# One 512-column width for two output products, modulation sums of two groups at a time, pool factors loaded ahead, low parts last

## The chip, the core and the metric

The kernel runs on one core of a Trainium2 chip. Its engines are PE (TensorE, matrix products; PEld is its weight load), DVE (VectorE), ACT (ScalarE), POOL (GpSimd) and SP (SyncE, which here only issues DMAs). Each runs its own program in order and waits for others by semaphores. The metric is device time in microseconds of one execution; lower is better. Before the change it is 2888.54 us (median of 3 runs, 2886.82 to 2889.20).

## What is computed

All arrays are float32. `first_block` runs two layers over two streams, 256 tokens of `x` and 256 of `ctx`, 2048 wide; the second layer returns only `x`. `second_block` then works on 256 tokens. Cut to what matters here:

```python
for l in range(2):
    sh, sc, g = split(silu(c) @ w_mod[l] + b_mod[l], 3)       # and the same of c_ctx, for the stream ctx
    parts = split((x * (1 + sc) + sh) @ w_in[l])              # cu cb cc cg q k v ag pu pg
    ...                                                       # attention, short convolution
    # pool, four groups, window w = 2, 4, 8, 16:
    mean = (csum[hi] - csum[lo]) / (hi - lo)                  # the divisors depend on the position alone
    y_pool = silu(pg) * (((mean - pu) @ pool_w[l]) * pool_scale[l])
    out = concat(y_conv, y_attn, y_pool) @ w_out[l]           # 2048 x 2048
    x = layernorm(ALPHA * x + g * out, ln_g[l], ln_b[l])
z = rms_norm(x) @ w_in_2                                      # second block: two kinds of attention, gates
x = x + merged @ w_out_2                                      # 2048 x 2048
x = x + square(relu(rms_norm(x) @ w_up_2)) @ w_down_2
return rms_norm(x)
```

## The kernel before

**Products.** A float32 number is carried as two fp32r parts, `hi` and `lo` (the rest), and a product is the sum of three: high by high and both cross terms. Weights come from HBM on SP's queue in chunks of 512 KB (128 x 1024 numbers, `fetch`, L181), some chunks ahead of use; for each, ACT makes `hi` (L184) and DVE makes `lo` (L185). `wget` hands out the next chunk.

`lin_a` keeps a tile of 128 tokens as the stationary operand and streams weight columns past it; for each chunk and tile it calls `mm3` for each of the chunk's rows of 128 (k). `lin_b` keeps weights as the stationary operand, four blocks of 128 columns a product, and streams the activations. With both streams (512 tokens) it calls `mm3`. With 256 tokens ("fold") it streams the activations' high and low parts side by side, 512 columns, past the weights' high part (L266), and then 256 columns past the weights' low part (L268). All matrix products of layer 1 and of block 2 that go through `lin_b` are of this kind: 368 chunks with eight such pairs each, in 50 products.

**Output products.** `BLOCKS` cuts the 2048 output columns of `w_out` (both layers), `w_out_2` and the last quarter of `w_down_2` into three blocks of 512 and two of 256. A 512-column chunk holds two k, a 256-column chunk four. `mix_out` consumes each block on DVE with three operations for each token tile (L830 to L832: times the gate, plus the residual, statistics), and after the last block computes the layer norm's factors and starts the next layer (its turns by PE at L947, scale and shift L952 and L954, split into high and low L350 and L351, and POOL's rows L1014 and L1015). In layer 0 that is four tiles, in layer 1 and in block 2 two.

**Modulation sums.** `silu(c) @ w_mod` for later layers is summed beside other work: `mod_side` reads a group of 512 columns in eight chunks; DVE multiplies and adds for each k and stream (L416, L418, into the tiles `ma0` and `ma1`), and when all 16 k are in, PE adds over the partitions with a matrix of ones (`cols` L428 or `gate` L446: one 32-row float32 matmul for each stream). `cols` has a copy and four transposes behind it (L430, L435), `gate` an addition for each stream and two DMAs. Ten calls of `cols` and eight of `gate` go this way, the last four of `gate` for one stream alone (`side2`, layer 1's gate for `x`). What is `deferred` runs some side steps later (a step a chunk), wherever in the product that is.

**Pool stage.** `do_pu` builds window sums on DVE, loads the 1/count factors with a DMA on ACT's queue for each of the four groups (L628), multiplies and subtracts into `tmp` tiles (L631, L632), and defers a float32 product with `pool_w` on PE (L636) by 3+b side steps.

A scheduler with a cost model of its own orders each engine's instructions; the program's text gives the dependencies and the buffers.

Of the kernel before, what the change touches and what calls it, by code (L numbers as in the profile page):

```python
# [19 lines left out]
P = 128  # L20
# [41 lines left out]
def tile_two_blocks(ctx: ExitStack, tc: tile.TileContext, a: dict, out: bass.AP, blocks: dict):  # L62
# [14 lines left out]
    p_qs = pool("qs", 10)  # L77
# [167 lines left out]
    def mm3(ps, lh, ll, rh, rl, start, stop):  # L245
        mm(ps, lh, rh, start=start, stop=False)  # L246
        mm(ps, lh, rl, start=False, stop=False)  # L247
        mm(ps, ll, rh, start=False, stop=stop)  # L248

    def lin_b(act, tok, consume, ncols=512, korder=K16, mid=None):  # L250
# [6 lines left out]
        for k0 in korder:  # L257
            hi, lo = wget()
            last = k0 == korder[-1]
            nk = hi.shape[1]  # L260
            for (c, w), p in zip(nb, ps):
                for kk in range(nk):
                    ah, al = act[k0 + kk]
                    start, stop = k0 == korder[0] and kk == 0, last and kk == nk - 1
                    if fold:
                        mm(p[:w, :].rearrange("p (a t) -> p a t", a=2), hi[:, kk, c:c + w], act.both(k0 + kk, tok),  # L266
                           start=start, stop=False)
# [3 lines left out]
                if last:  # L271
                    consume(c // P, (p[:w].rearrange("p (a t) -> p t a", a=2),) if fold else p[:w, :ntok])
            side()
            bg_step()
            if mid:
                mid(k0)

    def lin_a(act, tiles, consume, korder=K16, mid=None, hold=1, lead=0, hook=None):
# [4 lines left out]
        for ks in [korder[:lead]][:lead] + [[k] for k in korder[lead:cut]] + [korder[cut:]]:  # L283
# [5 lines left out]
            for i, t in enumerate(tiles):  # L289
                for k0, (hi, lo) in zip(ks, ws):  # L290
                    nk, n = hi.shape[1:]
                    for kk in range(nk):
                        ah, al = act[k0 + kk]
# [109 lines left out]
    def mod_side(l, nt, streams=(0, 1), wait=5):  # L403

        st = {}

        def fn(k0):
            def step(raw):
                if k0 == 0:
                    for s in streams:  # L410
                        st[s] = p_ma.tile([P, 512], F32, tag=f"ma{s}", name=f"ma{s}")
                for kk in range(CHUNK):
                    k = k0 + kk
                    for s in streams:
                        if k == 0:
                            V.tensor_scalar(st[s], raw[:, kk, :], cc2[:, k, s:s + 1], None, op0=ALU.mult)  # L416
                        else:
                            V.scalar_tensor_tensor(st[s], raw[:, kk, :], cc2[:, k, s:s + 1], st[s], op0=ALU.mult,  # L418
                                                   op1=ALU.add)
                if k0 == K16[-1]:  # L420
# [3 lines left out]

        def cols():
            ps = aux()
            for s in streams:
                mm(ps[32 * s:32 * s + 32, :], ones, st[s], start=True, stop=True)  # L428
            r = st[0][:64]
            S.copy(r, ps[:64])  # L430

            def finish():
                pt = aux()[:, :256].rearrange("p (b r) -> p b r", b=4)
                for b in range(4):
                    nc.tensor.transpose(pt[:, b, :], r[:, b * P:(b + 1) * P], ident[:64, :64])  # L435
                set_cols(l, nt // 4, nt % 4 * 4, 4, pt.rearrange("p b (s t) -> p b s t", s=2)[:, :, :, 0])
            deferred.append([2, finish])

        def gate():
            o = (nt - 8) * 512  # L440
            br = tmp()
            S.dma_start(br[:64], bass.AP(tensor=a["b_mod"].tensor, offset=a["b_mod"].offset + l * 3 * D + 2 * D + o,
                                         ap=[[0, 64], [1, 512]]))
            ps = aux()
            for s in streams:
                mm(ps[32 * s:32 * s + 32, :], ones, st[s], start=True, stop=True)  # L446
            for s in streams:
                V.tensor_add(br[32 * s:32 * s + 32], ps[32 * s:32 * s + 32, :], br[32 * s:32 * s + 32])
                S.dma_start(grow[l][s:s + 1, o:o + 512], br[32 * s:32 * s + 1])
        return entries(("w_mod", l), nt * 512, 512, K16, fn)  # L450
# [5 lines left out]
    NTS = [nt for j in range(4) for nt in (j, 4 + j)]  # L456
# [9 lines left out]
    def block_entries(name):  # L466
        return [e for c0, n in BLOCKS for e in entries(name, c0, n, KB[n], nk=CHUNK * 512 // n)]

    side0 = [e for nt in range(8, 12) for e in mod_side(0, nt)]
    side1 = [e for nt in NTS for e in mod_side(1, nt)]  # L470
    side2 = [e for nt in range(8, 12) for e in mod_side(1, nt, (1,))]
# [44 lines left out]
    def layer(l, hT, **first):  # L516
# [90 lines left out]
        def do_pu(_):  # L607
            pw = p_at.tile([P, 512], F32, tag="aT", name="pw", bufs=5).rearrange("p (g d) -> p g d", g=4)
            nc.sync.dma_start(pw, a["pool_w"][l].rearrange("g c d -> c g d"))
# [808 lines left out]
```

## Time and profile before

| what | us |
|---|---|
| median of 3 runs | 2888.54 (2886.82 to 2889.20) |
| the profiled execution | 2888.59 |
| its span, first to last instruction | 2886.8 |
| PE busy | 2857.0 (99%) |
| DVE busy | 2003.2 (69%) |
| ACT busy | 1159.7 (40%) |
| POOL busy | 222.5 (8%) |
| DMA, mean of the span | 185 GB/s |

The span is the stretch between the first and last instruction; 1.8 us of the execution lie outside it. Busy shares are means over stages that may have different limits. [...]

### The profile page before, as it was taken

The numbers are of one execution on the slowest core, as the hardware profiler recorded it, in microseconds if no ns is written. First come the engines' busy times: TensorE is split into PE (matmuls) and PEld (weight loads), VectorE is DVE, ScalarE is ACT, GpSimd is POOL, SyncE is SP. The second block draws the span as 40 slices with busy tenths as digits, with TensorE's granted clock in tenths as the row PEclk, the third lists the DMA queues.
The fourth block names the chain that finished last, engine by engine and source line by source line (L and its number), as shares of the span: only waits on it lengthen the run. The fifth ranks groups of instructions, "written<-read, shape, count | busy, mean of one in ns | idle before, by whom it ended". The sixth has DMA issues, their size and how long they took to land.

```text
span 2886.8 us, 39022 instructions
## 1 busy us (share of the span) xinstructions
PE 2857.0 (99%) x14970; PEld 2371.6 (82%) x14970; DVE 2003.2 (69%) x3061; ACT 1159.7 (40%) x1620; POOL 222.5 (8%) x284
## 2 busy tenths in 40 slices
PE   8999999999999999999999999999999999999998
PEld 6777787777879788888888888888888888888887
DVE  5889987887975658467676666776656656565564
ACT  3223432432312435245445443544444444344443
POOL 0000001001100410011100000001101001010011
PEclk9999999999999999999999999999999999999999
DMA  9764455445764445445756555455656656656555
GB/s 332 275 211 142 135 173 165 147 163 178 246 197 134 135 137 194 157 161 192 244 168 194 182 157 188 156 188 184 204 183 189 191 189 188 194 181 196 190 188 168
DMA packets 150532, 533.89 MB, mean 185 GB/s; under 512 B 17204, under 2 KB 21052, under 8 KB 149320
## 3 DMA queue, kind: packets, MB, share of 16 engines
q1 hardware_dynamic: 142752, 510.79, 54.3%
q0 software_dynamic: 5632, 18.36, 2.1%
q10 hardware_dynamic: 1960, 2.24, 0.3%
q8 instruction: 117, 1.92, 0.3%
q14 instruction: 71, 0.58, 0.1%
HBM read 527.09 MB, written 4.23 MB: 184 GB/s over the span
## 4 chain that ended last, share of the span: by engine, by line
PE 76%; DVE 2%; issue 2%; DMA 1%; ACT 1%; POOL 0%; POOLq 0%; ACTq 0%; DVEq 0%
PE acc L266 23%; PE acc L246 12%; PE acc L248 12%; PE acc L247 12%; PE acc L268 12%; PE aux L670 1%; PE aux L702 1%; DVE lo L185 1%; DVE ma L418 1%; PE aux L692 0%; PE aux L1184 0%; ACT hi L184 0%; DMA raw<-in_w_in_dram 0%; DMA raw<-in_w_out_dram 0%; PE aux L1214 0%
## 5 line engine op out<-in xcount | busy, mean ns | idle before, releaser
L185 DVE TENSOR_TENSOR lo<-raw,hi 128x1024 fp32r<-128x1024 f32 (+1 forms) x774 | 947.0, 1226 | 646.3 <-ACT hi L184 645.2
L184 ACT CAST hi<-raw 128x1024 fp32r<-128x1024 f32 (+1 forms) x774 | 808.4, 1045 | 1419.1 <-PE acc L248 447.8
L266 PE MATMUL acc<-act,hi 128*128 128x512 f32 x2960 | 1048.1, 399 | 0.4 <-DVE qs L308 0.4
L268 PE MATMUL acc<-act,lo 128*128 128x256 f32 x2960 | 828.3, 280 | 0.0
L266 PEld LDWEIGHTS acc<-act,hi 128*128 128x128 f32 x2960 | 554.1, 187 | 139.7 <-issue 5.1
L246 PE MATMUL acc<-hi,act 128*128 128x512 f32 (+1 forms) x1568 | 584.2, 373 | 2.7 <-ACT act L350 1.7
L247 PE MATMUL acc<-lo,act 128*128 128x512 f32 (+1 forms) x1568 | 578.6, 369 | 1.1 <-DVE lo L185 1.1
L248 PE MATMUL acc<-hi,act 128*128 128x512 f32 (+1 forms) x1568 | 578.6, 369 | 0.1
L268 PEld LDWEIGHTS acc<-act,lo 128*128 128x128 f32 x2960 | 556.9, 188 | 1.9 <-DVE lo L185 0.3
L418 DVE SCALAR_TENSOR_TENSOR ma<-mod,cc,ma 128x512 f32<-128x512 f32 x480 | 339.5, 746 | 26.2 <-DMA mod<-in_w_mod_dram 24.8
L246 PE MATMUL acc<-act,hi 128*128 128x512 f32 x896 | 356.9, 398 | 0.2 <-ACT hi L184 0.2
L247 PE MATMUL acc<-act,hi 128*128 128x512 f32 x896 | 350.2, 391 | 0.0
L248 PE MATMUL acc<-act,lo 128*128 128x512 f32 x896 | 350.1, 391 | 0.0
L246 PEld LDWEIGHTS acc<-hi,act 128*128 128x128 f32 x1568 | 296.5, 189 | 56.9 <-issue 4.0
L248 PEld LDWEIGHTS acc<-hi,act 128*128 128x128 f32 x1568 | 296.2, 189 | 51.5 <-DVE act L351 1.5
L247 PEld LDWEIGHTS acc<-lo,act 128*128 128x128 f32 x1568 | 296.6, 189 | 50.5 <-DVE lo L185 2.5
L246 PEld LDWEIGHTS acc<-act,hi 128*128 128x128 f32 x896 | 168.6, 188 | 46.1 <-issue 8.8
L248 PEld LDWEIGHTS acc<-act,lo 128*128 128x128 f32 x896 | 168.5, 188 | 35.9 <-issue 0.4
L247 PEld LDWEIGHTS acc<-act,hi 128*128 128x128 f32 x896 | 168.7, 188 | 33.5 <-issue 0.5
L317 DVE TENSOR_REDUCE tmp<-acc 128x256 f32<-128x512 f32 x185 | 124.3, 684 | 57.3 <-PE acc L268 57.3
L1292 POOL TENSOR_TENSOR tmp<-tmp 128x256 f32<-128x256 f32 x64 | 53.0, 828 | 573.3 <-DVE tmp L1291 566.6
L678 ACT ACTIVATE pp<-aux,small 128x512 f32<-128x512 f32 (+1 forms) x96 | 58.3, 613 | 55.1 <-DVE small L674 55.0
(217 smaller groups left out, 1655.0 us busy)
## 6 DMA issues: line engine op xcount, KB each, us to landing
raw<-in_w_in_dram SPq DMA_DIRECT2D x379, 512.0 KB, 4.0
mod<-in_w_mod_dram SPq DMA_DIRECT2D x152, 512.0 KB, 3.7
raw<-in_w_up_dram SPq DMA_DIRECT2D x128, 512.0 KB, 4.1
raw<-in_w_down_dram SPq DMA_DIRECT2D x128, 512.0 KB, 4.2
raw<-in_w_out_dram SPq DMA_DIRECT2D x96, 512.0 KB, 4.3
mod<-in_w_mod_dram SPq DMA_DIRECT2D x8, 2048.0 KB, 13.5
raw<-in_w_proj_a_dram SPq DMA_DIRECT2D x16, 512.0 KB, 4.1
raw<-in_w_proj_b_dram SPq DMA_DIRECT2D x16, 512.0 KB, 4.3
```

Of the source, the lines that this page charges most:

```text
L184: S.copy(hi, raw)
L185: (fn or V).tensor_sub(lo, raw, hi)
L246: mm(ps, lh, rh, start=start, stop=False)
L247: mm(ps, lh, rl, start=False, stop=False)
L248: mm(ps, ll, rh, start=False, stop=stop)
L266: mm(p[:w, :].rearrange("p (a t) -> p a t", a=2), hi[:, kk, c:c + w], act.both(k0 + kk, tok), start=start, stop=False)
L268: mm(p[:w, :ntok], lo[:, kk, c:c + w], ah[:, tok], start=False, stop=stop)
L317: V.reduce_sum(t, ps[0], axis=AX.X)
L418: V.scalar_tensor_tensor(st[s], raw[:, kk, :], cc2[:, k, s:s + 1], st[s], op0=ALU.mult, op1=ALU.add)
L670: mm(p[:, :nk], a[r, q0:q0 + P], b[r, 0:nk], start=n == 0, stop=n == 2)
L678: S.activation(t, ps[i][:, :nk], AF.Exp, bias=nm[:, i:i + 1], scale=QK_SCALE, accum_out=sums[:, i:i + 1])
L1292: G.tensor_mul(t, t, t)
```

## The change

1. `mm3` goes. In `lin_a`, for each chunk and tile, the products with the weights' `hi` come first for both (or all four) k, and those with `lo` behind them. In `lin_b`, the first and last chunk of a product do so for each block of 128 columns, and all chunks between for the four blocks together: eight products with `hi` (sixteen with 512 tokens), then eight with `lo`.
2. `WIDE` cuts layer 0's `w_out` and `w_out_2` into four blocks of 512 columns. Layer 1's `w_out` and the last `w_down_2` keep `BLOCKS`.
3. `mod_side` takes a list of groups. For `side0`, `side1` and `side2` it takes two at a time: their sums go to two to four row groups of one PSUM tile, with one copy, four transposes (of 128 x 128 with four rows of groups), or one gate addition behind them. `ma2` and `ma3` are new tiles; the pool `qs` gets 9 buffers instead of 10, and `fc` lies on `ma0`.
4. The 1/count factors are loaded by SP, two loads of 256 KB a layer ahead of the pool's product, into two of the five `aT` buffers; the multiply and subtract work in place in the `qs` tile, and the product with `pool_w` is deferred by 8+b side steps.

The core of the diff:

```diff
-    p_qs = pool("qs", 10)
+    p_qs = pool("qs", 9)
...
-            for (c, w), p in zip(nb, ps):
-                for kk in range(nk):
...
-                        mm(p[:w, :ntok], lo[:, kk, c:c + w], ah[:, tok], start=False, stop=stop)
-                    else:
-                        mm3(p[:w, :ntok], hi[:, kk, c:c + w], lo[:, kk, c:c + w], ah[:, tok], al[:, tok], start, stop)
...
+            pairs = list(zip(nb, ps))
+            for g in ([[x] for x in pairs] if last or k0 == korder[0] else [pairs]):
+                for (c, w), p in g:
+                    for kk in range(nk):
+                        ah, al = act[k0 + kk]
+                        wt, start = hi[:, kk, c:c + w], k0 == korder[0] and kk == 0
+                        if fold:
+                            mm(p[:w, :].rearrange("p (a t) -> p a t", a=2), wt, act.both(k0 + kk, tok), start=start,
+                               stop=False)
...
+                for (c, w), p in g:
+                    for kk in range(nk):
+                        mm(p[:w, :ntok], lo[:, kk, c:c + w], act[k0 + kk][0][:, tok], start=False,
+                           stop=last and kk == nk - 1)
...
-                        mm3(ps[i][:, :n], ah[:, t * P:(t + 1) * P], al[:, t * P:(t + 1) * P], hi[:, kk], lo[:, kk],
-                            k0 == korder[0] and kk == 0, k0 == korder[-1] and kk == nk - 1)
+                        for j, x in enumerate(act[k0 + kk]):
+                            mm(p, x[:, tt], hi[:, kk], start=k0 == korder[0] and kk == j == 0, stop=False)
+                    for kk in range(nk):
+                        mm(p, act[k0 + kk][0][:, tt], lo[:, kk], start=False, stop=k0 == korder[-1] and kk == nk - 1)
...
-                if k0 == K16[-1]:
+                if (nt, k0) == (nts[-1], K16[-1]):
                     deferred.append([wait, cols if nt < 8 else gate])
...
+        def sums():
+            ps = aux()
+            for j, job in enumerate(jobs):
+                mm(ps[32 * j:32 * j + 32, :], ones, st[job], start=True, stop=True)
+            return ps
...
-            for s in streams:
-                V.tensor_add(br[32 * s:32 * s + 32], ps[32 * s:32 * s + 32, :], br[32 * s:32 * s + 32])
-                S.dma_start(grow[l][s:s + 1, o:o + 512], br[32 * s:32 * s + 1])
...
+            V.tensor_add(br[:n], ps[:n], br[:n])
...
+    WIDE = [(512 * j, 512) for j in range(4)]
...
-    side1 = [e for nt in NTS for e in mod_side(1, nt)]
-    side2 = [e for nt in range(8, 12) for e in mod_side(1, nt, (1,))]
+    side0 = [e for nt in (8, 10) for e in mod_side(0, (nt, nt + 1))]
+    side1 = [e for j in range(4) for e in mod_side(1, (j, 4 + j))]
+    side2 = [e for nt in (8, 10) for e in mod_side(1, (nt, nt + 1), (1,))]
...
+            for b in (0, 2):
+                t = p_at.tile([P, 512], F32, tag="aT", name="ic", bufs=5)
+                nc.sync.dma_start(t, bass.AP(tensor=a["invc"].tensor, offset=a["invc"].offset + b * T,
+                                             ap=[[0, P], [1, 2 * T]]))
...
-                ic = tmp(T)
-                S.dma_start(ic, bass.AP(tensor=a["invc"].tensor, offset=a["invc"].offset + b * T,
-                                        ap=[[0, P], [1, T]]))
-                dd = tmp(NT)
-                V.tensor_mul(sh(dd), cur[:, :, o:o + T], ic[:, None, :].to_broadcast([P, ns, T]))
-                V.tensor_sub(sh(dd), sh(dd), u[:, :, 8:264])
+                dd = cur[:, :, o:o + T]
+                V.tensor_mul(dd, dd, ic[:, None, :].to_broadcast([P, ns, T]))
+                V.tensor_sub(dd, dd, u[:, :, 8:264])
...
-                deferred.append([3 + b, finish])
+                deferred.append([8 + b, finish])
```

In a row of the order, `acc` and `aux` are PSUM tiles, `act` activations, `hi` and `lo` weights, `ma_...` a tile of running modulation sums, and `x2` at the end two alike in a row. PE in block 2, inside a product of 256 tokens, before:

```order
L268 MATMUL acc<-act,lo 128x256
L266 MATMUL acc<-act,hi 128x512
L268 MATMUL acc<-act,lo 128x256
L266 MATMUL acc<-act,hi 128x512
L268 MATMUL acc<-act,lo 128x256
```

and now:

```order
L271 MATMUL acc<-act,lo 128x256 x2
L264 MATMUL acc<-act,hi 128x512 x2
L271 MATMUL acc<-act,lo 128x256 x2
L264 MATMUL acc<-act,hi 128x512 x2
L271 MATMUL acc<-act,lo 128x256 x2
L264 MATMUL acc<-act,hi 128x512 x8
L271 MATMUL acc<-act,lo 128x256 x8
L264 MATMUL acc<-act,hi 128x512 x8
L271 MATMUL acc<-act,lo 128x256 x8
```

The two kinds took turns one by one; now they come in twos in the first chunk of a product and in eights in the next. PE in layer 0, at a call of `cols` ahead of six score products of the attention, before:

```order
L246 MATMUL acc<-act,hi 128x512
L247 MATMUL acc<-act,hi 128x512
L248 MATMUL acc<-act,lo 128x512
L428 MATMUL aux<-ma_4268,ones 32x512
L428 MATMUL aux<-ma_4269,ones 32x512
L670 MATMUL aux<-qs 128x512 x6
L246 MATMUL acc<-act,hi 128x512
```

and now:

```order
L268 MATMUL acc<-act,hi 128x512
L271 MATMUL acc<-act,lo 128x512 x2
L437 MATMUL aux<-ma_3921,ones 32x512
L437 MATMUL aux<-ma_3922,ones 32x512
L437 MATMUL aux<-ma_4262,ones 32x512
L437 MATMUL aux<-ma_4263,ones 32x512
L692 MATMUL aux<-qs 128x512 x6
L724 MATMUL aux<-p_3610,aT 128x128
```

Two matmuls with `ones` in a call have become four, of the sums of two groups. DVE at the end of layer 0's output product, where one of the four tiles is consumed, before:

```order
L831 SCALAR_TENSOR_TENSOR p_7583<-p_7583,tmp 128x256
L832 BN_STATS bn<-p_7583 128x6
L185 TENSOR_TENSOR lo<-raw,hi 128x1024 x2
L830 TENSOR_TENSOR tmp<-acc,row 128x256
L831 SCALAR_TENSOR_TENSOR p_7577<-p_7577,tmp 128x256
L832 BN_STATS bn<-p_7577 128x6
L841 BN_AGGR small<-bn 128x2
L842 TENSOR_SCALAR small<-small 128x1
L844 SCALAR_TENSOR_TENSOR small<-small 128x1
L938 TENSOR_SCALAR p_6651<-p_6651,small 128x512
```

and now:

```order
L426 SCALAR_TENSOR_TENSOR ma_8909<-mod,cc_115,ma_8909 128x512
L185 TENSOR_TENSOR lo<-raw,hi 128x1024
L426 SCALAR_TENSOR_TENSOR ma_8909<-mod,cc_115,ma_8909 128x512 x4
L185 TENSOR_TENSOR lo<-raw,hi 128x1024
L426 SCALAR_TENSOR_TENSOR ma_8909<-mod,cc_115,ma_8909 128x512 x2
L185 TENSOR_TENSOR lo<-raw,hi 128x1024 x3
L853 TENSOR_TENSOR tmp<-acc,row 128x512
L854 SCALAR_TENSOR_TENSOR p_7535<-p_7535,tmp 128x512
L855 BN_STATS bn<-p_7535 128x6
L864 BN_AGGR small<-bn 128x2
```

The consuming operations are 512 columns wide, and additions of the second group of layer 1's gate sums (`ma_8909`), which stood some 40 chunks later, stand between the weights' low parts.

## Rows read from the trace of the kernel before

**Rows 1.** Page, parts 1 and 2: busy time by engine; TensorE's granted clock in 40 slices.

```profile
PE 2857.0 (99%) x14970; PEld 2371.6 (82%) x14970; DVE 2003.2 (69%) x3061; ACT 1159.7 (40%) x1620; POOL 222.5 (8%) x284
...
PEclk9999999999999999999999999999999999999999
```

**Rows 2.** Waits of PE: line waited for, total us, times, longest.

```profile
PE aux L670 <- ACT pp L678: 2.0, 1, 2.0
...
PE aux L636 <- DVE tmp L632: 0.8, 1, 0.8
```

**Rows 3.** Timeline of PE, whole 512-column stretch: start, length (us), operation.

```profile
2299.66 0.39 PE L246 MATMUL acc<-hi,act 128*128 128x512 f32 x1
...
2302.84 0.39 PE L248 MATMUL acc<-hi,act 128*128 128x512 f32 x1
```

**Rows 4.** Timeline of PE, 256-column blocks of the last product.

```profile
2869.73 0.28 PE L246 MATMUL acc<-hi,act 128*128 128x256 f32 x1
...
2872.97 0.28 PE L246 MATMUL acc<-hi,act 128*128 128x256 f32 x1
```

**Rows 5.** Timeline of PE, a call of sums for two streams, layer 0.

```profile
547.12 1.05 PE L428 MATMUL aux<-ma,ones 128*32 128x512 f32 x4
548.10 0.96 PE L670 MATMUL aux<-qs 64*128 64x512 f32 x6
```

**Rows 6.** Timeline of PE, a call of sums for one stream, layer 1.

```profile
1071.06 0.28 PE L268 MATMUL acc<-act,lo 128*128 128x256 f32 x1
1071.27 1.04 PE L446 MATMUL aux<-ma,ones 128*32 128x512 f32 x2
1072.25 1.19 PE L266 MATMUL acc<-act,hi 128*128 128x512 f32 x4
```

**Rows 7.** Timeline of PE, four column groups at once, near the start.

```profile
77.89 1.47 PE L379 MATMUL aux<-mod,csil 128*32 128x512 f32 x12
79.29 0.50 PE L246 MATMUL acc<-act,hi 128*128 128x512 f32 x1
```

**Rows 8.** Timeline of PE: four 64 x 64 transposes behind sums; four of 128 x 128 elsewhere.

```profile
717.38 0.46 PE L435 MATMUL aux<-ident,ma 64*128 64x64 f32 x4
...
959.05 0.60 PE L947 MATMUL aux<-ident,p 128*128 128x128 f32 x4
```

**Rows 9.** Stretches: window and its us, PE busy, clock, DMA share, GB/s.

```profile
510.00:516.00 6.00, 4.40 (x15) 0.72 0.60 188
968.00:974.00 6.00, 5.21 (x16) 0.72 0.89 306
```

**Rows 10.** Group of PE instructions, by shape: count, busy us, mean ns, idle before.

```profile
L266 PE MATMUL acc<-act,hi 128*128 128x512 f32 x2944 | 1042.4, 399 | 0.4 <-DVE qs L308 0.4
```

**Rows 11.** Timeline of PE, alternating products of 256 tokens, block 2.

```profile
2349.85 0.40 PE L266 MATMUL acc<-act,hi 128*128 128x512 f32 x1
...
2350.09 0.28 PE L268 MATMUL acc<-act,lo 128*128 128x256 f32 x1
...
2353.74 0.40 PE L266 MATMUL acc<-act,hi 128*128 128x512 f32 x1
```

**Rows 12.** Timeline of PE, two of one kind in a row, layer 1.

```profile
1385.59 0.64 PE L266 MATMUL acc<-act,hi 128*128 128x512 f32 x2
...
1386.06 0.28 PE L268 MATMUL acc<-act,lo 128*128 128x256 f32 x1
...
1386.41 0.40 PE L268 MATMUL acc<-act,lo 128*128 128x256 f32 x2
```

**Rows 13.** Groups of DVE instructions, shapes apart.

```profile
L418 DVE SCALAR_TENSOR_TENSOR ma<-mod,cc,ma 128x512 f32<-128x512 f32 x480 | 339.5, 746 | 26.2 <-DMA mod<-in_w_mod_dram 24.8
...
L830 DVE TENSOR_TENSOR tmp<-acc,row 128x512 f32<-128x512 f32 x18 | 11.6, 680 | 0.0
```

**Rows 14.** Timeline of DVE, end of layer 0's output product.

```profile
936.62 0.42 DVE L830 TENSOR_TENSOR tmp<-acc,row 128x256 f32<-128x256 f32 x1 [1.35 <-PE acc L248]
```

**Rows 15.** Timeline, all engines, just behind layer 0's output product.

```profile
958.32 6.39 DVE L351 TENSOR_TENSOR act<-tmp,act 128x512 fp32r<-128x512 f32 x2 [0.35 <-ACT act L350]
```

More of the change, by code (lines that the diff above doesn't have):

```diff
@@ L401, in mod_first, with mod_side, fn @@
         return res
-    def mod_side(l, nt, streams=(0, 1), wait=5):
+    def mod_side(l, nts, streams=(0, 1), wait=5):
+        jobs = [(nt, s) for nt in nts for s in streams]
         st = {}
-        def fn(k0):
+        def fn(nt, k0):
             def step(raw):
@@ L410, in step @@
                     for s in streams:
-                        st[s] = p_ma.tile([P, 512], F32, tag=f"ma{s}", name=f"ma{s}")
+                        j = jobs.index((nt, s))
+                        st[nt, s] = p_ma.tile([P, 512], F32, tag=f"ma{j}", name=f"ma{j}")
                 for kk in range(CHUNK):
@@ L423, in fn @@
             return step
-        def cols():
-            ps = aux()
-            for s in streams:
-                mm(ps[32 * s:32 * s + 32, :], ones, st[s], start=True, stop=True)
-            r = st[0][:64]
-            S.copy(r, ps[:64])
+        n = 32 * len(jobs)
+        def sums():
[3 more added lines that the diff above has]
+            return ps
+        def cols():
+            ps = sums()
+            r = st[jobs[0]][:n]
+            S.copy(r, ps[:n])
@@ L444, in gate @@
[L444 to L447, printed above, removed]
-                V.tensor_add(br[32 * s:32 * s + 32], ps[32 * s:32 * s + 32, :], br[32 * s:32 * s + 32])
-                S.dma_start(grow[l][s:s + 1, o:o + 512], br[32 * s:32 * s + 1])
-        return entries(("w_mod", l), nt * 512, 512, K16, fn)
+            for j, (nt, s) in enumerate(jobs):
+                o = (nt - 8) * 512
+                S.dma_start(br[32 * j:32 * j + 32],
+                            bass.AP(tensor=a["b_mod"].tensor, offset=a["b_mod"].offset + l * 3 * D + 2 * D + o,
+                                    ap=[[0, 32], [1, 512]]))
@@ L453, in tile_two_blocks @@
+            ps = sums()
+            V.tensor_add(br[:n], ps[:n], br[:n])
+            for j, (nt, s) in enumerate(jobs):
+                o = (nt - 8) * 512
+                S.dma_start(grow[l][s:s + 1, o:o + 512], br[32 * j:32 * j + 1])
+        return [e for nt in nts for e in entries(("w_mod", l), nt * 512, 512, K16, lambda k0, nt=nt: fn(nt, k0))]
     O = dict(cu=0, cb=512, cc=1024, cg=1536, q=2048, k=3072, v=4096, ag=5120, pu=6144, pg=6656)
@@ L816, in mix_out @@
         z = {}
-        stats = [p_sm.tile([P, len(BLOCKS), 6], F32, tag="bn", name="bn", bufs=4) for _ in tiles]
-        for m, (c0, n) in enumerate(BLOCKS):
+        blocks = WIDE if both else BLOCKS
+        stats = [p_sm.tile([P, len(blocks), 6], F32, tag="bn", name="bn", bufs=4) for _ in tiles]
+        for m, (c0, n) in enumerate(blocks):
             nt, o = divmod(c0, 512)
@@ L832, in c @@
                 V.bn_stats(stats[i][:, m, :], x)
-                if m == len(BLOCKS) - 1:
+                if m == len(blocks) - 1:
                     done(i, z, ln_coef(stats[i]))
-            lin_a(y, tiles, c, korder=KB[n], hold=HOLD if m == len(BLOCKS) - 1 else 1, hook=hook)
+            lin_a(y, tiles, c, korder=KB[n], hold=HOLD if m == len(blocks) - 1 else 1, hook=hook)
         return z
@@ L890, in plan_second @@
             plan(("w_proj_b_2",), 512 * j, 512, K8)
-        stream.extend(block_entries(("w_out_2",)))
+        stream.extend(block_entries(("w_out_2",), WIDE))
         for q in range(4):
@@ L908, in tile_two_blocks @@
             if n == 4:
-                m0, m1 = mod_side(0, nxt[0] // 4, wait=2), mod_first(1, *nxt, ("act",))
+                m0, m1 = mod_side(0, (nxt[0] // 4,), wait=2), mod_first(1, *nxt, ("act",))
                 m = m0[:4] + m1[:1] + m0[4:] + m1[1:]
@@ L918, in tile_two_blocks @@
             side0 = weave(w, side0, 1, 1)
-    rest = weave(layer_entries(0, L_REST) + block_entries(("w_out", 0)), side0 + side1, 1, 1)
+    rest = weave(layer_entries(0, L_REST) + block_entries(("w_out", 0), WIDE), side0 + side1, 1, 1)
     assert not rest
@@ L1140, in do_vv @@
         lin_a(hn, [0, 1], c, **(dict(lead=LEAD, hook=lead1) if (n, g) == ORDER2[0] else {}))
-    fc = cst.tile([P, T], F32, name="fc")
+    fc = p_ma.tile([P, 512], F32, tag="ma0", name="fc")[:, :T]
     fcol = cst.tile([P, 2, NH], F32, name="fcol")
@@ L1274, in tile_two_blocks @@
     hm = new_act(KT, 256)
-    for m, (c0, n) in enumerate(BLOCKS):
+    for m, (c0, n) in enumerate(WIDE):
         def c(i, ps):
@@ L1279, in c @@
             square_sum(t, ss[i], m)
-        lin_a(mg, [0, 1], c, korder=KB[n], hold=HOLD if m == len(BLOCKS) - 1 else 1)
+        lin_a(mg, [0, 1], c, korder=KB[n], hold=HOLD if m == len(WIDE) - 1 else 1)
         if (c0 + n) % 512 == 0:
```

46 lines of the change are left out of this document (20 added, 26 removed).

## Prediction

> **What bounds the kernel now.** I read the page first: PE is busy for 2857.0 of 2886.8 us, and its clock is granted in full in all 40 slices [rows 1]. DVE is next with 69%. So PE's own sequence sets the time: the change pays where it takes instructions from PE or shortens the step from one to the next, and on other engines it pays or costs only where PE then waits. Second I read PE's waits, which are few: the longest in mid kernel is 2.0 us at the first attention, and the pool stage has one of 0.8 [rows 2]. Third, the timeline of PE, for the step from one start to the next in every kind of stretch that the change touches; and last, DVE's groups and the stretch behind layer 0's output product, where DVE comes late.
>
> The sum is made against the profiled execution, 2888.6 us. The median of the runs is 2888.5, so nothing has to be carried over.
>
> **A. Four blocks of 512.** A 512-column product starts every 227 ns: 14 steps in 3.18 us [rows 3]. A 256-column one starts every 120 ns: 27 steps in 3.24 us [rows 4]. Two halves cost 240, one whole 227: 13 ns saved for a pair. In layer 0's `w_out` the last 512 columns are 4 tiles x 16 k x 3 products, 192 pairs; in `w_out_2` two tiles, 96. 288 x 13 ns = **-3.7 us**, all on PE's path. That is the trace's own price. [...]
>
> **B. Sums of two groups.** A float32 matmul of 512 columns leaves two records in the trace. A call for two streams, four records, takes PE from 547.12 to 548.10, 0.98 us [rows 5]; one for one stream, two records, from 1071.27 to 1072.25, 0.98 as well [rows 6]: two run side by side at the price of one. The second lies between fp32r products, and there the one ahead starts 0.21 us before the call, where its step is 0.12: 1.07 us a call. Would four cost more than two? At the start of the kernel four column groups of 32 run side by side: twelve records, three rounds of four, in 1.40 us [rows 7], 0.47 us a round, and a call has two rounds. So one with four should cost what one with two costs. The calls go from 18 (ten `cols`, eight `gate`) to 10 (six and four). 8 x 1.07 = **-8.6 us** (7.8 if only the 0.98 goes, 9.4 if the product behind loses 0.1 too).
>
> **C. Transposes behind the sums.** Ten `cols` become six, so four sets of four transposes go, at 0.46 us a set or somewhat less. The four sets that are left for pairs turn 128 x 128 instead of 64 x 64, 0.60 us instead of 0.46 [rows 8]. -1.8 + 0.6 = **-1.2 us** (-0.8 to -2.0, the latter with what each interruption costs around it).
>
> **D. Pool stage.** Layer 1's product waits 0.8 us for DVE's subtraction [rows 2], which itself stands behind the factors' load on ACT's queue. With the factors there ahead, and 8+b steps instead of 3+b, the wait goes, and with it what PE loses in starting again: **-1.3** (0 to -2.7). What is late next? The four loads of 256 KB go by SP, where the weights' loads wait behind them; at the 188 GB/s of an ordinary stretch [rows 9] that is 1.4 us each, within the cover of the chunks fetched ahead. If that cover were gone, 5.6 us.
>
> **E. Low parts last in products of 256 tokens.** 2944 pairs [rows 10] alternate now, and a pair takes 354 ns: eleven in 3.89 us; high to low is 0.24 of it, low to high 0.12 [rows 11]. By the code 268 of the 368 chunks lie inside a product, where 7 of 8 pairs will be followed by one of their kind; 100 are first or last, with 4 of 8: 1876 + 400 = 2276 pairs change. What do high after high and low after low cost? The trace has a few. Two high in a row start 0.47 us before the next low, of which high to low is 0.24, so high to high is 0.23; two low in a row last 0.12 longer than one [rows 12]. To ten ns that is 0.35, no answer. The uniform runs of `lin_a` give 227 + 120 = 347 [rows 3, 4]: 6.6 ns x 2276 = -15 us. The other end is a high that stays at 236 with a low that rises to 120: +2.4 ns, +5.5 us. The direct rows lie nearer to the uniform runs than to the bad end, but not surely below today's pair, and I take half: **-7.5 us**, the least certain term. In the 512-token products and in `lin_a` all steps are 227 already, and another order of equal widths should cost the same: 0.
>
> **F. Waits that move.** The 2.0 us at the first attention [rows 2] come because additions for the modulation sums, themselves waiting for their loads (24.8 us in all [rows 13]), stand on DVE ahead of the softmax's small steps; and PE's clock falls behind it, 0.72 granted in the 6 us there [rows 9], 1.7 us lost. The change puts the additions in other places, so these 3.7 us may go, or come again elsewhere: **-1** (-3.7 to +3.7).
>
> **G. Behind layer 0's output product.** The last block's consumers on DVE become 512 wide: 0.68 instead of 0.42 us each [rows 13, 14], three a tile, so +0.78 us a tile and +3.1 us for four. The additions for one more group of layer 1's gates come to stand there too: 16 x 0.746 = 11.9 us of DVE [rows 13]. PE has the next layer's first product meanwhile, but that needs activations and low parts from the same DVE, and PE is already short of them there (5.21 of 6 us busy, clock 0.72 [rows 9]). **+2**: -2 if a better interleaving spares that clock's fall, +7 if half of the 15 us reaches PE.
>
> Sum: -3.7 - 8.6 - 1.2 - 1.3 - 7.5 - 1 + 2 = -21.3, and 2888.6 - 21.3 = **2867 us**.
>
> **Rivals.**
> 1. *The order of low parts brings nothing* (E from 0 to +5.5). For it: 0.23 + 0.12 in the direct rows is not clearly less than 354. Against it: uniform runs are shorter in their sum. 2867 + 7.5 = 2875, up to 2880.
> 2. *It brings the whole of the uniform runs*: E = -15, so 2860, and with B and F at their better ends 2856; a little more with G's, 2854. For it: the direct 0.23 is that of the uniform 227. Against it: the high product here reads two stretches of activations, and nothing shows that its 236 comes from the alternation.
> 3. *DVE gets too late behind layer 0's output product.* Two operations there took 6.39 us instead of some 1.3 [rows 15], and the clock was at 0.72 just after. If the 11.9 + 3.1 us of new DVE work all end in waits of PE, with one more fall of the clock (1.7 us), that is +16.7 in place of +2: 2882. Against it: the additions wait for nobody on PE, and PE has four tiles of the next product as cover.
> 4. *The four sums do not run side by side*, and the change does not do what it says: six calls have four rows, each with another 0.98 us: +5.9, 2873. Against it: four column groups do so already, if with other operands [rows 7].
> 5. *Slower than before: DVE's waits for modulation loads reach PE.* DVE waits for them 24.8 us in all [rows 13], and the one wait of PE behind them today is the 2.0 us of F, with 1.7 for the clock: 3.7. Two groups' additions in one piece, their loads closer together, could put more such waits ahead of what PE needs, at the scores of the attention. Six more use up the 21 us; from eight on (29.6 us, so 2897) the kernel is slower by more than 0.2%. Against it: everywhere but at the attention PE has chunks ahead.
>
> **How the numbers follow.** Chances: the forecast (2860 to 2871) 0.46; rival 1, 0.20; rival 2, 0.14; rival 3, 0.09; rival 4, 0.05; rival 5, 0.06. The range leaves out rival 5, the upper half of rival 3 and the far ends of 1 and 2: 2854 to 2880. A difference under 0.2% (5.8 us) can hardly be told from none here, so below 2882.8 is faster, above 2894.3 slower. Faster: the forecast, rivals 1, 2 and 4, and half of rival 3, 0.89, less 0.02 for bad ends that meet: 0.87. Slower: most of rival 5, 0.05. Same: the rest, 0.08.
>
> **What will show it.** A: the 256-column groups of `lin_a` shrink from 960 to 384 instructions. B: a call with four rows and about 1 us to the next start; two would be rival 4. D: no wait of PE for the pool's subtraction. E: in a middle chunk eight high parts and eight low parts; 2.83 us for a chunk is rival 1, 2.78 the whole of the uniform runs. F and G: PE's waits at the first attention, and in the 40 us behind the end of layer 0's output product; more than 10 us of them there is rival 3. Half-clock stretches behind many waits at the attention would be rival 5. If the total misses by more than 12 us with A to D in place, E or G was mis-sized.

## The result, and the profile of the changed kernel

The changed kernel takes 2868.44 us (median of 4 runs, 2865.22 to 2870.06) where the kernel before takes 2888.87 beside it: a ratio of 0.9929, 95% interval 0.9912 to 0.9946, 20 us or 0.7% less. The forecast was 2867, with 2854 to 2880 as its range. The profiled execution took 2867.03 us, its span is 2865.3.

PE's line of the page, which answers to [rows 1], shows where the time went: PE is as full as before, with less to do.

```profile
PE 2831.1 (99%) x14666; PEld 2355.9 (82%) x14666; DVE 2005.7 (70%) x3039; ACT 1156.0 (40%) x1614; POOL 216.3 (8%) x284
```

The waits of PE (line waited for, total us, times, longest) answer to [rows 2]. The pool stage's 0.8 us has gone; the one at the first attention (L692, once L670) is there still; and two kinds have grown, of the turns by PE behind an output product (L970, 1.8 before) and of a product for its activations or its PSUM (L297):

```profile
PE aux L970 <- ACT tmp L975: 4.5, 3, 3.6
PE acc L297 <- ACT act L354: 2.8, 3, 1.4
...
PE aux L692 <- ACT pp L700: 1.9, 1, 1.9
PE acc L297 <- DVE tmp L321: 1.6, 1, 1.6
PE aux L970 <- DVE p L961: 1.3, 2, 0.7
```

The timeline of PE in block 2 (start, length, operation) answers to [rows 11]: eight high products in 1.84 us, eight low ones in 0.95, a chunk in 2.79 where eight pairs at 354 ns took 2.83.

```profile
2350.49 2.00 PE L264 MATMUL acc<-act,hi 128*128 128x512 f32 x8
2352.33 1.11 PE L271 MATMUL acc<-act,lo 128*128 128x256 f32 x8
2353.28 2.00 PE L264 MATMUL acc<-act,hi 128*128 128x512 f32 x8
2355.12 1.12 PE L271 MATMUL acc<-act,lo 128*128 128x256 f32 x8
2356.07 1.09 PE L264 MATMUL acc<-act,hi 128*128 128x512 f32 x4
```

A call of sums with four rows answers to [rows 5, 6]: eight records, and 0.99 us to the next start, where two rows took 0.98.

```profile
537.59 1.06 PE L437 MATMUL aux<-ma,ones 128*32 128x512 f32 x8
538.58 0.97 PE L692 MATMUL aux<-qs 64*128 64x512 f32 x6
```

And of 960 products of 256 columns in `lin_a` (three lines of 320), 384 are left (groups of PE by shape: count, busy us, mean ns, idle before):

```profile
L297 PE MATMUL acc<-hi,act 128*128 128x256 f32 x256 | 36.0, 283 | 0.0
...
L299 PE MATMUL acc<-lo,act 128*128 128x256 f32 x128 | 20.8, 284 | 0.0
```

**Where the 22 us went.** A record of a 512-column product is 0.39 us long where the next one starts 0.227 us behind its start [rows 3], so lengths overlap, and what a product takes of PE is read from start to start. Each start of a PE instruction was taken from the next one and the differences added up by kind of instruction, in both traces. Waits are in the sum of the instruction in front of the wait.

| kind | before, us | after, us | difference |
|---|---|---|---|
| 256-token products, high | 702.4 | 691.6 | -10.8 |
| 256-token products, low | 348.9 | 351.4 | +2.6 |
| `lin_a`, 256 columns | 116.4 (959 starts) | 47.0 (383) | -69.4 |
| `lin_a`, 512 columns | 867.1 (3744) | 935.6 (4032) | +68.5 |
| 512-token products | 628.4 | 626.8 | -1.6 |
| modulation sums | 17.6 | 9.9 | -7.8 |
| transposes behind sums | 3.5 | 2.4 | -1.2 |
| pool's product | 4.2 | 3.4 | -0.8 |
| all other | 183.6 | 182.0 | -1.6 |
| sum | 2872.2 | 2850.2 | -22.0 |

"All other" hides two sums that nearly cancel. The turns by PE behind output products (L947, now L970) take 19.2 us where they took 14.5, +4.7; the score products of the attention (L670, now L692) take 43.0 where they took 48.7, -5.7; the rest is -0.6.

**Behind layer 0's output product** something is lost. The stretch from 910 to 980 us holds that end in all the kernels here (window and its us, PE busy, clock, DMA share, GB/s). Before:

```profile
910.00:980.00 70.00, 66.16 (x425) 0.98 0.38 120
```

and after:

```profile
910.00:980.00 70.00, 63.19 (x294) 0.98 0.39 120
```

PE stands idle there for 6.8 us instead of 3.8. DVE at the longest of these waits (timeline):

```profile
946.63 0.99 DVE L977 TENSOR_SCALAR tmp<-aux,fs,fb 128x256 f32<-128x256 f32 x2
...
951.27 1.84 DVE L185 TENSOR_TENSOR lo<-raw,hi 128x1024 fp32r<-128x1024 f32 x1
953.03 6.18 DVE L355 TENSOR_TENSOR act<-tmp,act 128x512 fp32r<-128x512 f32 x1
959.14 1.21 DVE L185 TENSOR_TENSOR lo<-raw,hi 128x1024 fp32r<-128x1024 f32 x1
960.27 0.68 DVE L355 TENSOR_TENSOR act<-tmp,act 128x512 fp32r<-128x512 f32 x1
960.88 0.98 DVE L977 TENSOR_SCALAR tmp<-aux,fs,fb 128x256 f32<-128x256 f32 x2
```

and POOL at the same time:

```profile
946.68 1.30 POOL L1038 TENSOR_TENSOR p<-p,row 128x512 f32<-128x512 f32 x1
...
953.64 2.55 POOL L1037 TENSOR_TENSOR p<-p,row 128x512 f32<-128x512 f32 x2
956.15 2.51 POOL L1038 TENSOR_TENSOR p<-p,row 128x512 f32<-128x512 f32 x2
958.61 1.12 POOL L1039 DMA_DIRECT2D x<-p  x2
```

An operation of the same form takes DVE 0.68 us at 960.27 and 6.18 at 953.03, where it ends half a microsecond behind the last of four POOL operations. Two scalings (L977) stand behind it on DVE, ACT's part of the same work behind them, and PE waits (timeline of PE):

```profile
957.86 0.60 PE L970 MATMUL aux<-ident,p 128*128 128x128 f32 x4
962.06 1.11 PE L970 MATMUL aux<-ident,p 128*128 128x128 f32 x4 [3.60 <-ACT tmp L975]
962.83 2.05 PE L297 MATMUL acc<-hi,act 128*128 128x512 f32 x4
```

The four products at 962.83 take 2.05 us where four show 1.07 at 966.74. Behind the idle 3.60 us the granted clock is 0.50 (window and its us, PE busy, clock, DMA share, GB/s):

```profile
963.00:964.50 1.50, 1.50 (x5) 0.50 0.61 150
```

The operation of 6.39 us for two in [rows 15] is the same thing before the change; the prediction had read it as load of DVE.

**Behind layer 1's output product** something less is lost as well, for which the trace shows 0.8 us of idle time and 1.6 us by the clock, from 1470 to 1510 us (columns as above). Before:

```profile
1470.00:1510.00 40.00, 37.05 (x260) 1.00 0.49 157
```

and after:

```profile
1470.00:1510.00 40.00, 36.23 (x202) 0.96 0.43 136
```

### The profile page after: what moved, and what is told of

The parts are those of the page before. It is cut to its first block, busy times and chain, and to the rows that moved or that the text cites. A ratio compares the mean times of both kernels' runs of the same rounds, so it can differ in the third digit from the quotient of the medians.

```text
span 2865.3 us, 38384 instructions
## 1 busy us (share of the span) xinstructions
PE 2831.1 (99%) x14666; PEld 2355.9 (82%) x14666; DVE 2005.7 (70%) x3039; ACT 1156.0 (40%) x1614; POOL 216.3 (8%) x284
## 4 chain that ended last, share of the span: by engine, by line
PE 86%; DVE 6%; issue 3%; DMA 3%; ACT 1%; POOL 1%; SPq 0%; POOLq 0%; ACTq 0%; DVEq 0%
PE acc L264 23%; PE acc L297 18%; PE acc L271 18%; PE acc L299 9%; PE acc L267 6%; PE acc L268 6%; DMA mod<-in_w_mod_dram 2%; DVE ma L426 2%; DVE lo L185 1%; PE aux L692 1%; PE aux L724 1%; PE aux L383 1%; PE aux L714 1%; ACT hi L184 0%; DMA p<-in_ln_b_dram 0%
## 5 line engine op out<-in xcount | busy, mean ns | idle before, releaser
L185 DVE TENSOR_TENSOR lo<-raw,hi 128x1024 fp32r<-128x1024 f32 (+1 forms) x774 | 950.9, 1232 | 664.7 <-ACT hi L184 593.4
L264 PE MATMUL acc<-act,hi 128*128 128x512 f32 x2960 | 799.3, 395 | 0.2 <-DVE tmp L321 0.2
L297 PE MATMUL acc<-hi,act 128*128 128x512 f32 (+1 forms) x2944 | 768.1, 384 | 4.6 <-ACT act L354 2.8
L271 PE MATMUL acc<-act,lo 128*128 128x256 f32 (+1 forms) x3856 | 708.2, 306 | 0.0
L271 PEld LDWEIGHTS acc<-act,lo 128*128 128x128 f32 x3856 | 611.9, 189 | 92.5 <-DVE lo L185 0.3
L297 PEld LDWEIGHTS acc<-hi,act 128*128 128x128 f32 x2944 | 535.2, 189 | 114.6 <-ACT act L354 3.9
L264 PEld LDWEIGHTS acc<-act,hi 128*128 128x128 f32 x2960 | 508.9, 188 | 74.8 <-issue 1.5
L299 PE MATMUL acc<-lo,act 128*128 128x512 f32 (+1 forms) x1472 | 438.3, 382 | 1.0 <-DVE lo L185 1.0
L267 PE MATMUL acc<-act,hi 128*128 128x512 f32 x896 | 357.4, 399 | 0.2 <-ACT hi L184 0.2
L268 PE MATMUL acc<-act,hi 128*128 128x512 f32 x896 | 351.2, 392 | 0.0
L267 PEld LDWEIGHTS acc<-act,hi 128*128 128x128 f32 x896 | 168.9, 188 | 43.9 <-issue 7.3
L268 PEld LDWEIGHTS acc<-act,hi 128*128 128x128 f32 x896 | 169.0, 189 | 34.1 <-issue 0.7
L792 DVE TENSOR_TENSOR p<-acc,p 128x512 f32<-128x512 f32 x100 | 66.3, 684 | 12.0 <-PE acc L271 10.8
L355 DVE TENSOR_TENSOR act<-tmp,act 128x256 fp32r<-128x256 f32 (+1 forms) x107 | 68.4, 645 | 6.0 <-ACT act L354 6.0
L561 POOL TENSOR_TENSOR tmp<-p,cs 128x256 f32<-128x256 f32 x32 | 28.0, 883 | 500.5 <-DVE p L792 243.6
```

What stands on the lines that cost most here:

```text
L185: (fn or V).tensor_sub(lo, raw, hi)
L264: mm(p[:w, :].rearrange("p (a t) -> p a t", a=2), wt, act.both(k0 + kk, tok), start=start, stop=False)
L267: mm(p[:w, :ntok], wt, ah[:, tok], start=start, stop=False)
L268: mm(p[:w, :ntok], wt, al[:, tok], start=False, stop=False)
L271: mm(p[:w, :ntok], lo[:, kk, c:c + w], act[k0 + kk][0][:, tok], start=False, stop=last and kk == nk - 1)
L297: mm(p, x[:, tt], hi[:, kk], start=k0 == korder[0] and kk == j == 0, stop=False)
```

## The experiments

All ratios are to the kernel before, run beside each; where two kernels are compared with one another, their ratios are, and two of them carry some 0.002 (6 us) of uncertainty between them, so that the trace has to carry the smaller differences.

**The old order of products in the changed kernel.** `lin_b` and `lin_a` as before, with `mm3`:

```diff
-            pairs = list(zip(nb, ps))
-            for g in ([[x] for x in pairs] if last or k0 == korder[0] else [pairs]):
...
+            for (c, w), p in zip(nb, ps):
+                for kk in range(nk):
```

> The changed kernel with the old order of products (high, high, low for each k in the 512-wide steps; high and low in turns with 256 tokens), all else as changed. Theory (term E): the pair of a 512-column and a 256-column product goes back from about 351 ns to about 354, so PE's sequence is 7 to 8 us longer: 2868.4 + 7.5 = 2876. Rival (the order brings nothing, and the trace's difference is paid back by waits): within 2 us of 2868.4.

Measured: 2877.97 us, ratio 0.9964 (0.9951 to 0.9978), 0.0035 or 10 us above the changed kernel. The steps are the old ones again (timeline of PE, eight pairs in 2.83 us):

```profile
2353.09 0.40 PE L266 MATMUL acc<-act,hi 128*128 128x512 f32 x1
...
2355.92 0.40 PE L266 MATMUL acc<-act,hi 128*128 128x512 f32 x1
```

So the order is worth its step: by starts, the 256-token products take 11.0 us more in this run, waits included. PE's waits for the weights' low part rise from 1.0 to 5.9 us in it (4.7 in `lin_a`, 1.2 in `lin_b`).

**The order alone, on the kernel before.** The same edit the other way round.

> The kernel before with the new order of products alone (low parts last), nothing else of the change. Theory (term E): 2888 less 7 to 10 us, 2878 to 2881, the pair of a 512- and a 256-column product at 351 ns. Rival: the gain in the step is given back by waits that the other parts of the change took away, above all of the pool stage, where in the changed kernel with the old pool stage PE waits 6.9 us for the subtraction: then 2883 to 2886.

Measured: 2883.3 us, ratio 0.998 (0.9971 to 0.9989), 6 us less than before. That is at the near end of the rival's 2883 to 2886 and 2 us above the theory's. PE waits 2.3 us for the pool stage's subtraction where it waited 0.8, which is a part of what the rival said. Whether the order is worth less here than in the changed kernel, where undoing it cost 10 us, the intervals can't tell.

**Sums of one group at a time.**

```diff
-    side0 = [e for nt in (8, 10) for e in mod_side(0, (nt, nt + 1))]
+    side0 = [e for nt in range(8, 12) for e in mod_side(0, (nt,))]
```

and the like for `side1` and `side2`.

> The changed kernel with the modulation sums of one group at a time in all three places, so 18 calls instead of 10 and four sets of transposes more. Theory (terms B and C): 8 x 1.07 + 1.2 = +9.8, so 2878. Rival (four rows cost more than two, 0.98 us a call more): the changed kernel would have had only 3.9 of these, so 2872. If the additions of the second group that now stand behind layer 0's output product cost PE more than 2 us there, that comes off: 2874 to 2876.

Measured: 2879.64 us, ratio 0.9969 (0.9956 to 0.9981), 0.0040 or 11 us above the changed kernel; its profiled execution, 2876.36, is 9.3 above that of the changed one. The 9.8 of terms B and C stand, and four rows at the price of two.

**One group at a time for layer 1's gates only.** `side2` alone as above.

> The changed kernel with only layer 1's gate sums (one stream) back to one group at a time. It has two more calls of sums, +2.1 us, and two additions; the additions of the second group (11.9 us of DVE) leave the end of layer 0's output product. Theory (second half of term G small): 2870.5. Rival (these additions are what makes the wide block's consumers late): 2870.5 - 5 = 2865.5.

Measured: 2868.86 us, ratio 0.9935 (0.9922 to 0.9947): no difference from the changed kernel that could be told. PE's waits for the turns behind layer 0's output product are the same 4.5 us, longest 3.6. The last addition of a modulation sum ahead of the end of layer 0's output product starts before 870 us in this run and before 900 us in the changed kernel. So the additions of the second group are not what makes these waits.

**The pool stage as before.** The four loads on ACT's queue, `tmp` tiles, 3+b steps.

```diff
-                deferred.append([8 + b, finish])
+                deferred.append([3 + b, finish])
```

> The changed kernel with the pool stage as before: the factors loaded by ACT's queue for each group, products in tmp tiles, the product with pool_w deferred by 3+b steps. Theory (term D): PE's wait for the subtraction, 0.8 us, comes back, +1.3: 2869.7. Rival (what the changed trace suggests: there PE waits 1.6 us at 1391 us for DVE's reduction of the last pool gates, which before it did not): that wait goes as well, and the time is 2868 or 1 us less.

Measured: 2871.29 us, ratio 0.9949 (0.9935 to 0.9962), 0.0020 above the changed kernel, at the edge of what the two intervals can tell. The trace is plain: the wait that comes back is not 0.8 us (timeline of PE in layer 1):

```profile
1379.31 1.22 PE L652 MATMUL aux<-tmp,pw 128*128 128x256 f32 x2 [4.86 <-DVE tmp L648]
```

and 6.9 us in two waits in all. So neither expectation had the mechanism: among the other changes the old pool stage waits longer than it did in the kernel before. The new one spares that, and leaves 1.6 us of a later wait, which this run does not have.

**Layer 0's output product in blocks of 512 and 256 again.**

```diff
-        blocks = WIDE if both else BLOCKS
+        blocks = BLOCKS
```

> The changed kernel with layer 0's output product in three blocks of 512 and two of 256 columns, as before; w_out_2 stays in four of 512. Theory (terms A and G as forecast): +2.5 for 192 pairs of halves, less 2 for consumers on DVE that are narrow again: within 1 us of 2868.4. Rival: the wide last block is what makes PE wait longer behind this product in the changed kernel (some 7 us of waits between 925 and 963 us), which then go: 2868.4 + 2.5 - 6 = 2865. Second rival: the wide block costs nothing there: 2871.

Measured: 2863.4 us, ratio 0.9914 (0.9901 to 0.9928), 4 to 5 us less than the changed kernel by medians and ratios, which is within the uncertainty of the two; the profiled executions differ by 2.2 us. The rival's 2865 is nearest, and the trace bears it out. PE's busy time and clock in the stretch from 910 to 980 us:

```profile
910.00:980.00 70.00, 67.61 (x391) 1.00 0.39 128
```

PE is idle for 4.4 us less than with wide blocks, and the clock is 1.00 instead of 0.98, 1.4 us in 70: more than the 2.5 us that the pairs of halves cost. In layer 0 the wide blocks lose. For `w_out_2`, which no run took alone, nothing in the trace stands against their 1.3 us: from 2270 to 2345 us PE is busy without a gap at a clock of 1.00.

**POOL's rows later, by ten chunks.** Eight products and eight sums that write layer 1's residual are held back: a small copy by ACT out of a later weight chunk writes the tile into which their factors are loaded.

```diff
+        for _ in range(10):
+            yield
         for nt in range(4):
-            g, b = row(a["ln_g"], nt * 512), row(a["ln_b"], nt * 512)
+            g, b = (p_pp.tile([P, 512], F32, tag="pp", name="row") for _ in range(2))
+            hi = next(r for r in ready if not callable(r[1]))[0]
+            for t, nm in ((g, "ln_g"), (b, "ln_b")):
+                S.copy(t[:, :8], hi[:, 0, :8])
+                row(a[nm], nt * 512, t)
```

> The changed kernel with POOL's sixteen products and sums of layer 0's normalized rows (the ones that write the residual for layer 1) held back by about ten chunks of weights: their row factors are loaded into tiles that a small ACT copy of a later weight chunk writes first. Theory: DVE operations behind layer 0's output product that take 5 to 6 us instead of 0.7 do so because POOL works at the same time; without POOL there PE's waits between 925 and 963 us (3.6 us the longest) and the fall of the clock behind them shrink, -4 to -7 us: 2862 to 2865. Rival: DVE has simply too much to do there, or the long operations wait for ACT or for a buffer: within 2 us of 2868.4.

Measured: 2875.18 us, ratio 0.9956 (0.9944 to 0.9969), 7 to 8 us *more* than the changed kernel. Behind layer 0's output product it did what the theory says (from 910 to 980 us PE is busy for 67.64 us instead of 63.19, at a clock of 1.00); the loss came elsewhere. The timeline around 1050 us, of POOL, DVE and PE:

```profile
1047.72 2.51 POOL L1043 TENSOR_TENSOR p<-p,row 128x512 f32<-128x512 f32 x2 [4.93 <-DMA row<-in_ln_g_dram]
...
1050.19 2.48 POOL L1044 TENSOR_TENSOR p<-p,row 128x512 f32<-128x512 f32 x2
...
1053.21 1.41 POOL L561 TENSOR_TENSOR tmp<-p,cs 128x256 f32<-128x256 f32 x2
1053.98 1.27 DVE L562 TENSOR_TENSOR p<-tmp 128x256 f32<-128x256 f32 x2 [6.25 <-POOL tmp L561]
...
1055.90 1.22 PE L264 MATMUL acc<-act,hi 128*128 128x512 f32 x2 [6.56 <-DVE p L312]
```

The rows now stood on POOL ahead of the rotation of layer 1's keys (L561), DVE waited 6.25 us for that, a reduction stood behind it on DVE, and PE waited 6.56 us for the PSUM tile that it reads. The forecast of -4 to -7 was right on the place and had not asked who else waits for POOL.

**POOL's rows later, by two chunks.** The same with `range(2)`.

> The changed kernel with POOL's sixteen products and sums of layer 0's normalized rows held back by two chunks instead of ten, so that they fall where layer 1's first product runs on PE and DVE has one operation in 5.4 us. In the run with ten chunks the long DVE operations and PE's waits between 940 and 960 us had gone, but a wait of 6.6 us came at 1056 us, where POOL then met DVE at the attention's inputs. Theory: POOL at work makes DVE's operations long wherever the two meet; with two chunks they meet at neither place: 2868.4 less 4 to 7, 2862 to 2864. Rival: the ACT copies and later loads that hold POOL back are themselves the price: 2868 or more.

Measured: 2860.54 us, ratio 0.9906 (0.9892 to 0.9919), 6 to 8 us less than the changed kernel. The stretch from 910 to 980 us:

```profile
910.00:980.00 70.00, 67.67 (x325) 1.00 0.27 91
```

DVE's group of the operation that had taken 6.18 us, from 930 to 975 us (count, busy us, mean ns, idle before), in the changed kernel:

```profile
L355 DVE TENSOR_TENSOR act<-tmp,act 128x512 fp32r<-128x512 f32 x15 | 22.8, 1545 | 1.4 <-ACT act L354 1.4
```

and here:

```profile
L355 DVE TENSOR_TENSOR act<-tmp,act 128x512 fp32r<-128x512 f32 x14 | 9.3, 688 | 1.1 <-ACT act L354 1.1
```

DVE's operations are 0.69 us each. What was moved is POOL's rows, with the loads of their factors and the stores of their results: the DMA traffic of the stretch falls from 120 to 91 GB/s too, and eight small ACT copies are new. The part on the prediction, below, tells these apart by all the traces.

**Both: blocks of 512 and 256 in layer 0, and POOL's rows later by two chunks.**

> Layer 0's output product in three blocks of 512 and two of 256 columns, and POOL's sixteen operations held back by two chunks as well, all else as changed. If the wide last block and POOL's operations cost by the same path (PE waiting for late activations behind layer 0's output product), the two gains share: about 2861, 2 below the better one alone. If they are separate: 2863.4 - 5 = 2858.

Measured: 2858.22 us, ratio 0.9898 (0.9884 to 0.9912), with the last one below the fastest here, 9 to 10 us less than the changed kernel and 30 less than the one before. PE is idle for 0.9 us in the stretch:

```profile
910.00:980.00 70.00, 69.15 (x403) 1.00 0.29 91
```

The time is the 2858 of the second expectation, but that had put the gain of the rows at 5 us. With what they gained alone, 8, separate gains of 5 and 8 would give 2855 to 2856. The trace shows that the two share: alone they bring the idle time from 6.8 us to 2.4 and to 2.3, together to 0.9. With POOL's rows moved, what is left between wide and narrow blocks can't be told: 2 us by medians, and the profiled executions, 2857.46 and 2858.42, are the other way round.

**POOL's rows later, alone, on the kernel before.**

> The kernel before with POOL's sixteen products and sums of layer 0's normalized rows held back by two chunks, as in the run on the changed kernel. Theory: the collision of POOL and DVE was there before the change (an operation of 5.8 us at 958 us, then waits of 1.1, 0.9 and 0.9 us and a fall of the clock), so this alone gains 4 to 6 us: 2883. Rival: only the wide last block makes it cost: within 2 us of 2888.

Measured: 2882.14 us, ratio 0.9981 (0.9972 to 0.999), 5.5 us less. The collision was there before the change:

```profile
910.00:980.00 70.00, 69.22 (x460) 1.00 0.26 83
```

**The fastest kernel with the old order in `lin_a` alone.** `mm3` in `lin_a`, `lin_b` as changed.

> The best kernel so far (layer 0's output product in three blocks of 512 and two of 256, POOL's sixteen operations two chunks later, else as changed, 2858.2) with the old order of products in lin_a alone: for each k high by high, high by the weights' low part, the activations' low part by high. lin_b keeps the new order. Theory: all of the order's gain is in lin_b's step from one product to the next, and lin_a's new order only asks two k of activations sooner; behind layer 1's output product PE lost 3.5 us with the old order and 5.4 to 6.7 with the new one, so -2 to -3: 2855 to 2856. Rival: lin_a's new order is what spares PE the waits for the weights' low part (4.7 us in five in the run with the old order everywhere): +2 to +4: 2860 to 2862.

Measured: 2858.15 us, ratio 0.9899 (0.9883 to 0.9916): the same. Neither expectation came, and with two intervals of this width a difference under 6 us could not be told: PE's waits for weights' low parts are 0.9 us, and what it saves behind layer 1's output product (some 1 us more of PE busy between 1470 and 1510 us) shows up again at the attention. So no gain of the new order in `lin_a` is to be seen; what was measured of it is in `lin_b`.

## Why the prediction was right, and where its steps were not

The total came within 2 us. The terms that carry it, B, C and E, were sized from steps between starts on the engine that bounds the kernel, and they stand. The rest is in part luck: losses and gains that no term has, or that a term had in another place, nearly cancel.

- **A** (-3.7) and **G** (+2). The count of products is what the code said, and their steps are unchanged, 227 and 120 ns in both traces. Even so `lin_a` gave only 0.9 us, and the turns behind output products cost 4.7; together +3.8. Four things of known size make up 3.3 of that: A's -3.7, the 1.6 us of a wait at 1391 us (see D), 3.0 us more of idle time behind layer 0's output product, which is G, and 2.4 behind layer 1's, which no term has (the rows above). G's size was near, and its mechanism wrong in one half: the additions of the second group, 11.9 of its 15 us, cost nothing that could be told (the run with `side2` alone); the wide blocks do. Undone alone, layer 0's two thirds of A turn out to cost 3 to 5 us: 2.5 gained by width, some 6 lost behind it. That they cost because what follows them slides under POOL's rows fits the run with both edits, where with the rows moved no cost can be told; the intervals leave it open within 6 us. Rival 3 named the place and took DVE's long operation for load; it was a collision.
- **B** and **C** (-9.8): -7.8 and -1.2 by starts, and 9 to 11 by the run without them. Right, including the reading that four rows cost what two do, which rival 4 denied.
- **D** (-1.3): the product's own sum fell by 0.8, the wait of 0.8 us went (it stood in the rows of the 256-token products), and 1.6 us of another wait came at 1391 us, for the reduction of the pool gates. So D came to nothing. The step that asked what is late next looked at the loads alone. The new wait is absent from the run with the old pool stage and from the one with the old order, so it takes both parts; how they make it is not shown. Among the other changes the new stage is worth more than the forecast, since the old one would have waited 6.9 us.
- **E** (-7.5): -8.2 by starts, 0.8 of it D's wait. The high products gained 3.6 ns each and the low ones lost 0.9. The direct rows and the uniform runs of [rows 12, 3, 4] bracket it; that it came out in the middle was a choice between two ends and not worked out. Rivals 1 and 2 both fell.
- **F** (-1): the wait at the first attention is 1.9 us instead of 2.0, so nothing there. But the score products of all the attentions together take 5.7 us less, which the forecast had not seen. 4.0 of that go again with the old order and 1.4 with sums of one group at a time; how they come about no run shows. Rival 5 did not come.

What remains, -1.6 in the 512-token products and -0.6 in the rest, has no term, and no run was made for it.

That the long operation at 953 us is a matter of POOL and DVE at work together is shown by the runs that move POOL's rows, and by the traces of all 13 kernels taken together. Of the two forms that are stretched here (L185 with 1024 columns and L355 with 512), 9312 operations met no arithmetic of POOL, and none of them took over 1.3 times the median of its form. Of those that met some, 60 of 69 of L355's did, and 330 of 1019 of L185's. DMA traffic alone does not do it: from 50 to 200 us in the changed kernel, with 275 GB/s and no work of POOL, L185 takes 1.22 us and L355 0.68.

How the two meet isn't shown, nor what decides which operations it takes. In the traces before and after the change, of the operations that met arithmetic of POOL, 15 of 17 of L355's with 512 columns (L351 before) and 47 of 158 of L185's with 1024 took over 1.3 times the median of their form. Of the scalings that read PSUM (L977, once L954) none of 19 did: 0.99 us for two at 946.63 beside POOL's operation at 946.68, and 0.98 for two at 960.88, when POOL had ended. By the recorded starts the operation of 6.18 us (953.03) came ahead of the first of the four on POOL (953.64), and it lasted longer than any one of them: all four (2.55 + 2.51 us) had gone by before it ended.

## What to carry to other kernels

Read what a change is worth from start to start on the engine that is full. The order of instructions of different widths counts there as well: grouping equal ones gave some 3 ns in 354 on average, nearly three thousand times. At a place where that engine waits, look for an operation that takes several times the usual length before you call its engine overloaded: it may be another engine that must move, not the load. And when you move it, ask who else waits for the engine that does it; the same move cost 7 us with ten chunks and gained 7 with two.

## What was not expected of the hardware

One DVE operation of 0.68 us took 6.18 beside four POOL operations of 1.3 us each, and the same happened before the change (5.8 us at 958.32). Four row groups of 32 in one PSUM tile, from four `ones` products in a row, run side by side on PE: 0.99 us for four at 537.59, 0.98 for two and for one [rows 5, 6]. A product of 512 columns that takes activations of 256 tokens in two parts costs 230 ns in a run of its own kind (eight in 1.84 us at 2350.49) and 236 when it takes turns with one of 256 columns (the mean of eleven from 2349.85 before the change).
